# A decoder layer in fp32 on one core: the second weight unit in halves, later returns of turned rows, and a last norm whose shift rows come from TensorE

## The chip, the cores and the metric

The kernel runs on one core of a Trainium2 chip. The metric is the device time of one execution in microseconds (us). A core has a matmul engine (TensorE, PE in the profile; PEld is its weight load), three engines for elementwise work (VectorE or DVE, ScalarE or ACT, GpSimd or POOL) and a queue engine (SyncE, SP) that mostly issues DMA transfers. Each engine runs its own list of instructions in order and waits on semaphores that other engines or transfers raise.

## The reference

One layer, batch 1, 256 tokens, model width 2048, all in float32. Cut to what the change touches:

```python
h = layer_norm(ALPHA*h + 0.5*swiglu(h, ffn1...), ln1_g, ln1_b)
mix = mixer(h, ...)      # w_in, latent attention (MLA) and differential attention, gates, w_out
h = layer_norm(ALPHA*h + mix, ln2_g, ln2_b)
h = layer_norm(ALPHA*h + 0.5*swiglu(h, ffn2...), ln3_g, ln3_b)

def swiglu(x, w_gate, w_up, w_down): return (silu(x @ w_gate) * (x @ w_up)) @ w_down
def layer_norm(x, g, b):
    mu = mean(x); var = mean((x - mu)**2)
    return (x - mu) * rsqrt(var + 1e-5) * g + b
# inside the mixer
c_q, c_kv, k_r, dq, dk, dv, gate_mla, gate_diff = split(h @ w_in)
q = (rms_norm(c_q) @ w_uq) ...; k_nope = rms_norm(c_kv) @ w_uk; v = rms_norm(c_kv) @ w_uv
```

## The kernel before, in words

The 256 tokens are two blocks `b` of 128. A product of two fp32 matrices is done as three fp32r matmuls of 128x128 by 128x512 (`triple`, L208 to L210): high part times high part, high times low of the weight, low of the activation times high. High and low parts are made on the way: a weight comes by DMA on the SP queue into a `raw` tile (four buffers) or an `sraw` tile, ACT casts it (the high part, L154), DVE subtracts the cast from the raw values (the low part, L155), and the two land in a pair of tiles of a ring named `wring`. Activations pass through the same `split`, as `x`, `xs`, `cn`, `y`, `h`. PE's first use of a weight unit, L208, waits for the cast; the second, L209, for the subtraction. A unit is 128x1024, two k tiles.

The products of the FFNs and the mixer are mostly taken by `Hybrid`, with seven block products in the place of eight. In these DVE also forms sums of weight blocks (L428) and of products, and ACT copies PSUM banks into `snap` tiles (L385, L386), from which DVE later takes differences (L1194, with dk's rows as `dkTr`).

Work beside the matmuls is put into a list by `later(n, fn)`: it is emitted when n more units have been emitted (`tick`). After that a scheduler orders the instructions of each engine; `tc.issue_after(i)` holds what it wraps behind instruction i. The order on each engine is therefore fixed when the program is built.

A transposition of 128x512 rows goes by DVE (`blocks`, L715), four POOL-issued writes to DRAM (`turn`, L717), and one POOL-issued read (`turned`, L729, 256 KB), after which ACT copies or casts it. In the mixer the rows of the two latents wait in DRAM from an early stage on; `c_back` (L1227) reads them back as four `turned` tiles, and `cn.put` splits them (`cn`). `turned`, `blocks`, `gp` and the rows of `dkT` share one pool of six temporary tiles, so that each transfer into one waits until a former user is done.

The first projection (gate and up of FFN1) loads x transposed between its weight units: `load_x` (L1401) brings one quad of k tiles and one token block, 256 KB. Its first unit is loaded and split in two halves (`parts`).

The norms are a class. `evac` adds a bank to `z`, `bn_stats` and `bn_aggr` give mean and variance (`mv`), and `rstd` makes 1/sqrt in six small steps (`ve`, `sd` on ACT, `w`, `y`, `t`, `f`). In the last norm (no `cols`), `center(c)` does (z - mean) * g on a chunk of 512 columns (L833), a second pass does z * f + bias (L839), and each chunk is stored by SP at once (L1433). Chunks of z live in `z`, gains and biases in `gb`. LN2, whose `gained` brings ln1's gain and bias rows (`gp`) and applies them to the residual, runs beside w_out.

Of the kernel before, what the change touches and what calls it, by code (L numbers as in the profile page):

```python
# [18 lines left out]
P = 128  # L19
# [11 lines left out]
G = 2  # L31
# [28 lines left out]
def layer_kernel(ctx: ExitStack, tc: tile.TileContext, a: dict, out: bass.AP):  # L60
# [89 lines left out]

    cast, lows, fetched = [None], [None], [None]

# [59 lines left out]
    def project(w, x, k_tiles, width, done, k0=0, hook=None, between=None, norm=None, free=(3, 7)):  # L212
# [526 lines left out]
    class LayerNorm:  # L739
        def __init__(self, scale, residual, g, bt, each, x=None, cols=None, at=((0, 2, 4, 6), (8, 11, 14, 17)), ahead=None, pending=None, due=(), past=None):  # L740
# [45 lines left out]
            for n in range(4):  # L786
                later(at[0][n], lambda n=n: rows(n // 2, n % 2))
                if cols is None:
                    later(at[1][n], lambda n=n: vector(n // 2, n % 2))
            self.stats = [small.tile([P, 4, 6], F32, tag="bn", name=nm("bn"), bufs=4) for _ in range(2)]  # L790

# [32 lines left out]
        def apply(self, b):  # L824
# [3 lines left out]
            if self.cols is None:  # L828
# [3 lines left out]
                def center(c):  # L832
                    V.scalar_tensor_tensor(out=zs[c], in0=zs[c], scalar=mv[:, 0:1], in1=gs[c],  # L833
                                           op0=ALU.subtract, op1=ALU.mult)
                r = rstd(mv[:, 1:2], LN_EPS, 1, lambda: center(0))
                for c in range(4):
# [294 lines left out]
    def mixer(x):  # L1131
# [92 lines left out]
        def c_back():  # L1224
            for key, src in turns.items():
                back[key] = tmp_tile([P, 512], "turned")
                nc.gpsimd.dma_start(back[key], src)  # L1227
# [186 lines left out]
    def keep(i):  # L1414
        def each(b, c, z):
# [16 lines left out]
    ffn(2, h2, a["gu2"], a["dn2"], res[1], a["ln3_g"], a["ln3_b"],  # L1432
        lambda b, c, z: nc.sync.dma_start(out[b * P:(b + 1) * P, c * 512:(c + 1) * 512], z), norm=ln,  # L1433
        pending=(a["ln2_g"], a["ln2_b"]))
# [85 lines left out]
```

## Time and profile before

| | |
|---|---|
| median of 3 runs | 1966.95 us (1966.76 to 1967.80) |
| profiled execution | 1969.03 us |
| its span | 1967.3 us, so 1.7 us lie outside it |
| PE busy | 1951.7 us, 99% of the span, 8760 matmuls |
| DVE, ACT, POOL busy | 1777.8, 1249.7, 309.3 us |
| DMA | 488.83 MB, 248 GB/s over the span |
| mean granted clock of TensorE | 0.998 |

A row of a timeline reads: start in us from the span's start, duration, engine, source line, operation, output<-inputs, how many in a row, and in brackets the idle time of that engine just before and what ended it. Rows of the list of waits name who waited, for whom, the total in us, how many times, and the longest.

### The profile page before, as it was taken

The page shows a single profiled execution, that of the slowest core. Times are in us where ns is not written, and L with a number is a line of the kernel's source. Part 1 is how long each engine was busy: PE and PEld are TensorE (multiplying, and loading weights), DVE is VectorE, ACT ScalarE, POOL GpSimd, SP SyncE. Part 2 cuts the span into 40 slices and gives each one's busy share as a digit, 9 for nine tenths or more (in the row PEclk, how much of TensorE's full clock was granted, in tenths as well). Part 3 has the DMA queues.
Part 4 walks back from the last instruction along what each step waited for, and adds up shares of the span by engine and source line. Part 5 has one row for each costly group of instructions (what it writes and reads, how often), then busy time and mean ns, then how long its engine had stood idle before and what let it go on. Part 6 is the DMA issues. An engine that isn't in the chain of part 4 may idle for free.

```text
span 1967.3 us, 25772 instructions
## 1 busy us (share of the span) xinstructions
PE 1951.7 (99%) x8760; PEld 1618.2 (82%) x8760; DVE 1777.8 (90%) x2183; ACT 1249.7 (64%) x1634; POOL 309.3 (16%) x531
## 2 busy tenths in 40 slices
PE   9999999999999999999999999999999999999997
PEld 8888888888888898888888887888888888888886
DVE  7999999998998879988987676789999999999986
ACT  6666766676655666666667654556676666765661
POOL 0112111122100010102241530001211112210000
PEclk9999999999999999999999999999999999999999
DMA  8978888878776666767685788678888878787773
GB/s 315 285 227 262 268 261 247 259 234 306 271 238 214 208 223 248 246 223 262 203 248 196 236 295 274 198 261 255 255 267 264 250 238 271 251 314 236 277 233 121
DMA packets 149779, 488.83 MB, mean 248 GB/s; under 512 B 21600, under 2 KB 21648, under 8 KB 149648
## 3 DMA queue, kind: packets, MB, share of 16 engines
q1 hardware_dynamic: 119088, 401.13, 59.5%
q0 software_dynamic: 30560, 86.07, 16.8%
q8 instruction: 68, 1.11, 0.2%
q14 instruction: 63, 0.52, 0.1%
HBM read 456.71 MB, written 30.41 MB: 248 GB/s over the span
## 4 chain that ended last, share of the span: by engine, by line
PE 92%; DMA 3%; DVE 1%; issue 1%; ACT 1%; POOL 1%; SPq 0%; DVEq 0%; POOLq 0%; ACTq 0%
PE mm L209 29%; PE mm L208 29%; PE mm L210 29%; DMA turned<-turn 1%; DMA gate<-gates 1%; PE tr L210 1%; PE tr L209 1%; PE tr L208 1%; DMA turn<-blocks 0%; POOL turn L717 0%; PE tr L671 0%; ACT wring L154 0%; DMA raw<-in_wgd_dram 0%; DMA raw<-in_gu_dram 0%; PE tr L1322 0%
## 5 line engine op out<-in xcount | busy, mean ns | idle before, releaser
L154 ACT CAST wring<-raw 128x1024 fp32r<-128x1024 f32 (+2 forms) x467 | 481.9, 1037 | 322.3 <-PE mm L210 236.7
L155 DVE TENSOR_TENSOR wring<-raw,wring 128x1024 fp32r<-128x1024 f32 (+2 forms) x467 | 557.4, 1201 | 91.7 <-ACT wring L154 89.4
L154 ACT CAST wring<-sraw 128x1024 fp32r<-128x1024 f32 x436 | 453.0, 1052 | 201.9 <-DVE sraw L428 85.7
L155 DVE TENSOR_TENSOR wring<-sraw,wring 128x1024 fp32r<-128x1024 f32 x436 | 520.7, 1219 | 23.6 <-ACT wring L154 20.7
L208 PE MATMUL mm<-wring,h 128*128 128x512 f32 (+2 forms) x1248 | 480.9, 385 | 0.0
L210 PE MATMUL mm<-wring,h 128*128 128x512 f32 (+2 forms) x1248 | 480.3, 385 | 0.0
L209 PE MATMUL mm<-wring,h 128*128 128x512 f32 (+2 forms) x1248 | 480.0, 385 | 0.0
L208 PE MATMUL mm<-wring,xs 128*128 128x512 f32 x776 | 302.2, 389 | 0.6 <-ACT snap L385 0.6
L209 PE MATMUL mm<-wring,xs 128*128 128x512 f32 x776 | 301.9, 389 | 0.0
L210 PE MATMUL mm<-wring,xs 128*128 128x512 f32 x776 | 301.9, 389 | 0.0
L208 PEld LDWEIGHTS mm<-wring,h 128*128 128x128 f32 x1248 | 234.5, 188 | 46.9 <-ACT h L154 0.6
L209 PEld LDWEIGHTS mm<-wring,h 128*128 128x128 f32 x1248 | 234.5, 188 | 46.5 <-DVE wring L155 0.4
L210 PEld LDWEIGHTS mm<-wring,h 128*128 128x128 f32 x1248 | 234.4, 188 | 46.5 <-DVE h L155 0.7
L428 DVE TENSOR_TENSOR sraw<-sraw,sraw 128x1024 f32<-128x1024 f32 x168 | 199.2, 1219 | 2.0 <-DMA sraw<-in_wgm_dram 1.2
L208 PEld LDWEIGHTS mm<-wring,xs 128*128 128x128 f32 x776 | 145.7, 188 | 31.2 <-ACT snap L385 1.0
L210 PEld LDWEIGHTS mm<-wring,xs 128*128 128x128 f32 x776 | 145.7, 188 | 30.2
L209 PEld LDWEIGHTS mm<-wring,xs 128*128 128x128 f32 x776 | 145.7, 188 | 30.1
L717 POOL DMA_DIRECT2D hT<-blocks x176 | 96.8, 562 | 367.0 <-DVE blocks L715 366.0
L209 PE MATMUL mm<-wring,x 128*128 128x512 f32 x336 | 130.8, 389 | 0.5 <-DVE wring L155 0.5
L208 PE MATMUL mm<-wring,x 128*128 128x512 f32 x336 | 130.8, 390 | 0.0
L210 PE MATMUL mm<-wring,x 128*128 128x512 f32 x336 | 130.6, 389 | 0.0
L430 POOL DMA_DIRECT2D sraw<-in_gu_dram x40 | 35.5, 889 | 371.3 <-DVE sraw L428 288.3
(310 smaller groups left out, 2286.7 us busy)
## 6 DMA issues: line engine op xcount, KB each, us to landing
sraw<-in_gu_dram SPq DMA_DIRECT2D x160, 512.0 KB, 5.2
raw<-in_gu_dram SPq DMA_DIRECT2D x159, 512.0 KB, 4.9
raw<-in_dn_dram SPq DMA_DIRECT2D x140, 512.0 KB, 4.7
sraw<-in_gu_dram POOLq DMA_DIRECT2D x40, 512.0 KB, 7.1
sraw<-in_dn_dram SPq DMA_DIRECT2D x36, 512.0 KB, 5.2
eraw<-in_gu_dram SPq DMA_DIRECT2D x64, 256.0 KB, 5.8
raw<-in_w_out_dram SPq DMA_DIRECT2D x32, 512.0 KB, 4.3
hraw<-hT POOLq DMA_DIRECT2D x56, 256.0 KB, 5.8
```

The source lines that it names most:

```text
L154: cast[0] = S.copy(hi, src)
L155: lows[0] = V.tensor_tensor(out=lo, in0=src, in1=hi.bitcast(F32), op=ALU.subtract)
L208: PE.matmul(o, xh, wh, start=first, stop=False, skip_group_check=again)
L209: PE.matmul(o, xh, wl, start=False, stop=False, skip_group_check=again)
L210: PE.matmul(o, xl, wh, start=False, stop=last, skip_group_check=again)
L428: last = V.tensor_tensor(out=R[src][i], in0=R[src][i], in1=R[add[1]][i], op=ALU.add)
L430: nc.gpsimd.dma_start(R["12"][s], source("22", s), accum_op=ALU.add)
L717: nc.gpsimd.dma_start(to.rearrange("(g r) (i f) -> i r g f", g=4, i=4)[i], t[32 * i:32 * (i + 1), :].rearrange("r (g f) -> r g f", g=4))
```

## The change

It has four parts.

1. **Head.** The second weight unit of the first projection (j = 1) is loaded and split in halves too. The load of unit 3 is held behind the x load that was emitted last (`placed`).
2. **Mixer.** The read-back of the latents (`c_back`) moves from 6 to 12 units ahead, and the four splits into `cn` from 12 to 18 units (plus 4 and 2 per tile, as before).
3. **LN2.** The residual rows and the first two `gained` chunks come one unit later; the use of the first chunk's rows is due after 3 and 5 units, not 4 and 6.
4. **Tail.** For token block 1 of the last norm, chunks 0 and 1 of z are multiplied by the gain during FFN2 (`gained_ahead`). The last norm then needs, for these chunks, z*g * r minus a row (mean * r * g - bias). That row comes from TensorE: `ends` puts ln3's gain and bias, high and low parts, into rows of a 64-row tile (`gb_rows`); ACT builds a column pair (mean * r, and -1), PE transposes it, ACT copies it (`lhs`), and one matmul per chunk makes the shift in a PSUM bank. DVE then does one pass per chunk, from PSUM. Chunks go in the order 3, 2, 0, 1; chunk 1 in two halves, and the last half's store is issued from ACT's queue.

```diff
-            parts = [slice(i * width, (i + 1) * width) for i in range(G)] if between is not None and j == 0 else [slice(0, G * width)]
+            parts = [slice(i * width, (i + 1) * width) for i in range(G)] if between is not None and j < 2 else [slice(0, G * width)]
...
-                for c in parts:
-                    fetched[0] = nc.sync.dma_start(st["raw"][:, c], w[j][:, c])
+                with tc.issue_after(placed[0].ins) if between is not None and j == 3 else nullcontext():
+                    for c in parts:
+                        fetched[0] = nc.sync.dma_start(st["raw"][:, c], w[j][:, c])
...
-        nc.sync.dma_start(raw, a["xT"][q, b])
+        placed[0] = nc.sync.dma_start(raw, a["xT"][q, b])
...
-                later(4, lambda: use(0))
-                later(6, lambda: use(1))
+                wait = 3 if past is not None and c == 0 else 4
+                later(wait, lambda: use(0))
+                later(wait + 2, lambda: use(1))
...
+                def ends():
+                    raw = act_tile([P, 1024], F32, "gbraw")
+                    self.gb_rows = act_tile([P, 1024], F32R, "gbr")
+                    self.pair = tmp_tile([P, 64], "pair", F32R)
+                    V.memset(raw[0:64, :], 0.0)
...
+                    for i, v in ((0, g), (1, g), (2, bt), (32, g), (33, bt)):
+                        nc.gpsimd.dma_start(raw[i:i + 1, :], v[0:1, 0:1024])
+                    def parted():
+                        S.copy(self.gb_rows[0:64, :], raw[0:64, :])
+                        V.tensor_tensor(out=self.gb_rows[32:64, :], in0=raw[32:64, :],
+                                        in1=self.gb_rows[32:64, :].bitcast(F32), op=ALU.subtract)
+                    later(5, parted)
+                def gained_ahead(c):
+                    z = self.z[1][0][:, c * 512:(c + 1) * 512]
+                    with tc.issue_after(lows[0].ins):
+                        V.tensor_tensor(out=z, in0=z, in1=self.gb[0][0][:, c * 512:(c + 1) * 512], op=ALU.mult)
+                later(at[1][1] + 1, ends)
+                for c in range(2):
+                    later(at[1][0] + 5 + c, lambda c=c: gained_ahead(c))
...
+                if b == 1:
+                    r = rstd(mv[:, 1:2], LN_EPS, 1, lambda: center(3))
+                    s = sm(1, "s")
+                    S.activation(s, mv[:, 0:1], AF.Identity, scale=r)
+                    S.copy(self.pair[:, 0:33:32], s.to_broadcast([P, 2]))
+                    S.activation(self.pair[:, 1:2], self.pair[:, 0:1].bitcast(F32), AF.Identity, scale=-1.0, bias=s)
+                    t = tr_bank()
+                    PE.transpose(t[0:64, 0:P], self.pair.bitcast(F32), ident)
+                    lhs = tmp_tile([P, P], "lhs", F32R)
+                    S.copy(lhs[0:64, :], t[0:64, 0:P])
+                    shifts = [mm_bank() for _ in range(2)]
+                    for c in range(2):
+                        PE.matmul(shifts[c], lhs[0:64, :], self.gb_rows[0:64, c * 512:(c + 1) * 512], start=True, stop=True)
+                    for c in (3, 2, 0, 1):
...
-        later(6, c_back)
+        later(12, c_back)
...
-                later(12 + 4 * i + 2 * b, lambda i=i, b=b: cn.put(i, b, turned(back[i, b])))
+                later(18 + 4 * i + 2 * b, lambda i=i, b=b: cn.put(i, b, turned(back[i, b])))
...
-    ln = LayerNorm(1.0, res[0], a["ln2_g"], a["ln2_b"], keep(1), h2, a["ln2_cols"], ((1, 3, 11, 13), ()), 1,
-                   (a["ln1_g"], a["ln1_b"]), (2, 7, 14, 21), lambda: yq.made[3, 1])
+    ln = LayerNorm(1.0, res[0], a["ln2_g"], a["ln2_b"], keep(1), h2, a["ln2_cols"], ((2, 4, 11, 13), ()), 1,
+                   (a["ln1_g"], a["ln1_b"]), (3, 8, 14, 21), lambda: yq.made[3, 1])
```

Where instructions stand now, at three places.

The first is DVE in the head, around weight units 9 (`wring_103`, low part), 10 (`wring_121`) and 11 (`wring_119`); `sg` and `hb` are the gate's evacuation of the first projection, `xs` the activations' block sums. DVE before the change:

```order
L155 TENSOR_TENSOR wring_105<-raw_318,wring_104 128x1024
L155 TENSOR_TENSOR xs_337<-fa_288,xs_336 128x1024
L155 TENSOR_TENSOR wring_121<-raw_356,wring_120 128x1024
L870 TENSOR_TENSOR hb_306<-mm_136,sg_304 128x256
L155 TENSOR_TENSOR wring_103<-raw_340,wring_102 128x1024
L870 TENSOR_TENSOR hb_316<-mm_148,sg_314 128x256
L155 TENSOR_TENSOR wring_119<-raw_376,wring_118 128x1024
L155 TENSOR_TENSOR xs_373<-fb_289,xs_372 128x1024
L155 TENSOR_TENSOR wring_117<-raw_392,wring_116 128x1024
```

DVE at the same place after the change:

```order
L155 TENSOR_TENSOR wring_105<-raw_321,wring_104 128x1024
L155 TENSOR_TENSOR wring_121<-raw_359,wring_120 128x1024
L919 TENSOR_TENSOR hb_309<-mm_136,sg_307 128x256
L919 TENSOR_TENSOR hb_319<-mm_148,sg_317 128x256
L155 TENSOR_TENSOR xs_340<-fa_291,xs_339 128x1024
L155 TENSOR_TENSOR wring_119<-raw_379,wring_118 128x1024
L155 TENSOR_TENSOR wring_103<-raw_343,wring_102 128x1024
L155 TENSOR_TENSOR wring_117<-raw_395,wring_116 128x1024
L155 TENSOR_TENSOR xs_376<-fb_292,xs_375 128x1024
```

Unit 9's low part stood ahead of the second `hb`, of unit 11 and right behind the first `hb`; now the second `hb`, `xs_340` and unit 11 stand ahead of it.

The second is POOL's queue in the mixer, at the products of dv; `turn_7366`, `7409`, `7463`, `7470` (before) and `turn_7369`, `7412`, `7458`, `7465` (after) are dk's four row tiles on their way to `dkT`. POOL before the change:

```order
L717 DMA turn_7366<-blocks_7367 32x4x128 x4
L1227 DMA turned_7433<-turn_5559 128x512
L717 DMA turn_7409<-blocks_7410 32x4x128 x4
L1227 DMA turned_7435<-turn_5626 128x512
L1227 DMA turned_7437<-turn_6324 128x512
L1227 DMA turned_7439<-turn_6443 128x512
L729 DMA turned_7441<-turn_7366 128x512
L717 DMA turn_7463<-blocks_7464 32x4x128 x4
L717 DMA turn_7470<-blocks_7471 32x4x128 x4
L729 DMA turned_7499<-turn_7409 128x512
L729 DMA turned_7521<-turn_7463 128x512
L729 DMA turned_7523<-turn_7470 128x512
```

POOL at the same place after the change:

```order
L718 DMA turn_7369<-blocks_7370 32x4x128 x4
L730 DMA turned_7436<-turn_7369 128x512
L718 DMA turn_7412<-blocks_7413 32x4x128 x4
L730 DMA turned_7494<-turn_7412 128x512
L718 DMA turn_7458<-blocks_7459 32x4x128 x4
L718 DMA turn_7465<-blocks_7466 32x4x128 x4
L730 DMA turned_7516<-turn_7458 128x512
L730 DMA turned_7518<-turn_7465 128x512
L1276 DMA turned_7537<-turn_5562 128x512
L1276 DMA turned_7539<-turn_5629 128x512
L1276 DMA turned_7541<-turn_6327 128x512
L1276 DMA turned_7543<-turn_6446 128x512
```

The four reads of the latents (L1227, now L1276) stood among the writes of dk's rows and now stand behind all of them and their reads. With `dkT` made earlier, the scheduler also moved one matmul of the attention scores (L1299, `tr_7782`) forward on PE, from a later stage to between two of dv's products:

```order
L209 MATMUL mm_7475<-wring_119,xs_5877 128x512
L210 MATMUL mm_7475<-wring_118,xs_5877 128x512
L1299 MATMUL tr_7782<-dkT_7032,dqT_6758 128x128
L208 MATMUL mm_7499<-wring_116,xs_5766 128x512
L209 MATMUL mm_7499<-wring_117,xs_5766 128x512
L210 MATMUL mm_7499<-wring_116,xs_5767 128x512
L208 MATMUL mm_7499<-wring_116,xs_5766 128x512
L209 MATMUL mm_7499<-wring_117,xs_5766 128x512
```

Before, this piece of PE's list held the same products without the L1299 row, which then stood some 180 rows later.

The third is DVE at the end, for token block 1 of the last norm (`mm_15605` and `mm_15606` are the shift banks). DVE before the change:

```order
L826 BN_AGGR mv_15564<-bn_13735 128x2
L690 TENSOR_SCALAR ve_15566<-mv_15564 128x1
L833 SCALAR_TENSOR_TENSOR z_13981<-z_13981,mv_15564,gb_15261 128x512
L696 TENSOR_SCALAR w_15570<-mv_15564 128x1
L700 RECIPROCAL y_15573<-sd_15568 128x1
L833 SCALAR_TENSOR_TENSOR z_13981<-z_13981,mv_15564,gb_15261 128x512
L703 SCALAR_TENSOR_TENSOR t_15575<-y_15573,w_15570 128x1
L833 SCALAR_TENSOR_TENSOR z_14759<-z_14759,mv_15564,gb_15308 128x512
L709 SCALAR_TENSOR_TENSOR f_15577<-t_15575,y_15573 128x1
L833 SCALAR_TENSOR_TENSOR z_14759<-z_14759,mv_15564,gb_15308 128x512
L839 SCALAR_TENSOR_TENSOR z_13981<-z_13981,f_15577,gb_15358 128x512 x2
L839 SCALAR_TENSOR_TENSOR z_14759<-z_14759,f_15577,gb_15403 128x512 x2
```

DVE at the same place after the change:

```order
L852 BN_AGGR mv_15582<-bn_13738 128x2
L691 TENSOR_SCALAR ve_15584<-mv_15582 128x1
L859 SCALAR_TENSOR_TENSOR z_14762<-z_14762,mv_15582,gb_15311 128x512
L697 TENSOR_SCALAR w_15588<-mv_15582 128x1
L701 RECIPROCAL y_15591<-sd_15586 128x1
L704 SCALAR_TENSOR_TENSOR t_15593<-y_15591,w_15588 128x1
L710 SCALAR_TENSOR_TENSOR f_15595<-t_15593,y_15591 128x1
L879 SCALAR_TENSOR_TENSOR z_14762<-z_14762,f_15595,gb_15419 128x512
L859 SCALAR_TENSOR_TENSOR z_14762<-z_14762,mv_15582,gb_15311 128x512
L879 SCALAR_TENSOR_TENSOR z_14762<-z_14762,f_15595,gb_15419 128x512
L879 SCALAR_TENSOR_TENSOR z_13984<-z_13984,f_15595,mm_15605 128x512
L879 SCALAR_TENSOR_TENSOR z_13984<-z_13984,f_15595,mm_15606 128x256 x2
```

Two of four centering passes are gone, none stands between `y` and `f` any more, and the chunks 3 and 2 come first.

More of the change, by code (lines that the diff above doesn't have):

```diff
@@ L149, in at @@
             return self.tiles[k // 8, b][which][:, k % 8, :]
-    cast, lows, fetched = [None], [None], [None]
+    cast, lows, fetched, placed = [None], [None], [None], [None]
     def split(hi, lo, src):
@@ L789, in __init__ @@
                     later(at[1][n], lambda n=n: vector(n // 2, n % 2))
+            if cols is None:
+                def ends():
[3 more added lines that the diff above has]
+                    V.memset(raw[0:64, :], 0.0)
+                    V.memset(self.pair.bitcast(F32), 0.0)
+                    V.memset(self.pair[:, 2:34:31].bitcast(F32), -1.0)
+                    for i, v in ((0, g), (1, g), (2, bt), (32, g), (33, bt)):
[12 more added lines that the diff above has]
+                    later(at[1][0] + 5 + c, lambda c=c: gained_ahead(c))
             self.stats = [small.tile([P, 4, 6], F32, tag="bn", name=nm("bn"), bufs=4) for _ in range(2)]
@@ L834, in center @@
                                            op0=ALU.subtract, op1=ALU.mult)
+                if b == 1:
[12 more added lines that the diff above has]
+                    for c in (3, 2, 0, 1):
+                        if c == 2:
+                            with tc.issue_after(last.ins):
+                                center(2)
+                        for o in (slice(0, 512),) if c != 1 else (slice(0, 256), slice(256, 512)):
+                            last = V.scalar_tensor_tensor(out=zs[c][:, o], in0=zs[c][:, o], scalar=r,
+                                                          in1=(bs[c] if c > 1 else shifts[c])[:, o], op0=ALU.mult,
+                                                          op1=ALU.add if c > 1 else ALU.subtract)
+                            self.each(b, c, zs[c][:, o], o)
+                    return
                 r = rstd(mv[:, 1:2], LN_EPS, 1, lambda: center(0))
@@ L1432, in layer_kernel @@
     ffn(2, h2, a["gu2"], a["dn2"], res[1], a["ln3_g"], a["ln3_b"],
-        lambda b, c, z: nc.sync.dma_start(out[b * P:(b + 1) * P, c * 512:(c + 1) * 512], z), norm=ln,
+        lambda b, c, z, o=slice(0, 512): (nc.scalar if o.start else nc.sync).dma_start(
+            out[b * P:(b + 1) * P, c * 512 + o.start:c * 512 + o.stop], z), norm=ln,
         pending=(a["ln2_g"], a["ln2_b"]))
```

## The prediction

> **What bounds the kernel now.** I read the page first, then the list of PE's waits, then the windows of the stages that the change touches, and then their timelines.
>
> ```profile
> span 1967.3 us, 25772 instructions
> PE 1951.7 (99%) x8760; PEld 1618.2 (82%) x8760; DVE 1777.8 (90%) x2183; ACT 1249.7 (64%) x1634; POOL 309.3 (16%) x531
> ```
>
> PE is busy 99% of the span. No part of the change takes a matmul away (it adds three small ones at the end), so only the 15.6 us in which PE does not work can be won. The list of PE's waits names the longest of them inside the kernel; two windows, late in FFN2 and in the tail, follow:
>
> ```profile
> PE tr L671 <- DVE diff L1376: 1.8, 1, 1.8
> ...
> PE mm L208 <- ACT snap L385: 0.6, 1, 0.6
> PE mm L209 <- DVE wring L155: 0.5, 1, 0.5
> ...
> 1870.00:1952.00 82.00, 82.00 (x363) 67.89 (x362) 65.29 (x73) 39.21 (x42) 2.12 (x4) 1.00 0.55 182
> ...
> 1960.00:1964.00 4.00, 0.00 (x0) 0.00 (x0) 3.88 (x7) 0.00 (x0) 0.00 (x0) 0.50 0.32 118
> ```
>
> The four parts aim at the wait on `wring` (head), on `snap` (mixer), on `diff` (LN2) and the tail after PE's last matmul. In the windows the numbers after the length are the busy times of PE, PEld, DVE, ACT and POOL; the 1.00 or 0.50 near the end is TensorE's granted clock. The sum below is made against the profiled execution, 1969.03 us (span 1967.3 and 1.7 outside it); the median is 1966.95, 2.1 less, and I apply the differences to the median.
>
> **Head.** What the halves are to cure:
>
> ```profile
> 7.99 1.05 ACT L154 CAST wring<-raw 128x1024 fp32r<-128x1024 f32 x1 [0.84 <-DMA raw<-in_gu_dram]
> 9.07 2.49 DVE L155 TENSOR_TENSOR wring<-raw,wring 128x1024 fp32r<-128x1024 f32 x2 [1.20 <-ACT wring L154]
> 9.20 0.63 PE L208 MATMUL mm<-wring,x 128*128 128x512 f32 x2
> 9.26 1.05 ACT L154 CAST wring<-raw 128x1024 fp32r<-128x1024 f32 x1 [0.22 <-DMA raw<-in_gu_dram]
> 10.36 0.50 PE L209 MATMUL mm<-wring,x 128*128 128x512 f32 x1 [0.53 <-DVE wring L155]
> ```
>
> Unit 1 arrives at 7.99; its cast takes 1.05 and the subtraction some 1.24 more (2.49 for two), so PE's L209 starts at 10.36. The second L208 began at 9.43 (two in 0.63 us, a start every 0.23), and L209 would have been due at 9.66: 0.70 is lost, and 0.1 more in a slow restart. With halves, the low part of the first half follows its own arrival after about half of both durations, before PE is due. This wait goes: −0.8.
>
> Two things turn up instead. First, the x loads. The new SP order puts units 3, 4 and 5 ahead of x quad 2, where before only units up to 4 were ahead of it.
>
> ```profile
> 13.88 0.62 ACT L154 CAST x<-xraw 128x512 fp32r<-128x512 f32 x1 [1.21 <-DMA xraw<-in_xT_dram]
> 15.74 1.22 DVE L155 TENSOR_TENSOR wring<-raw,wring 128x1024 fp32r<-128x1024 f32 x1
> ```
>
> Unit loads arrive 1.27 us apart (7.99 and 9.26 above), so quad 2 comes at about 15.15, not 13.88. ACT waits there, unit 4's cast is behind it on ACT, and unit 4's low part, made 15.74 to 16.96 before, ends at about 18.23. PE used it at 18.45; with 0.8 less lost ahead of it, and one L208 more hoisted in front, it is due at 17.7 to 17.8. That is a wait of about 0.5 (0 if the transfers catch up, 0.8 if the last x half is late too).
>
> Second, unit 9. Its low part now stands on DVE behind the second `hb`, `xs_340` and unit 11, and that `hb` waits for an ACT `sg` that waits for the last matmul of the first gate bank:
>
> ```profile
> 27.95 0.38 ACT L863 ACTIVATE sg<-mm 128x256 f32<-128x256 f32 x1 [0.16 <-PE mm L210]
> 28.91 0.42 DVE L870 TENSOR_TENSOR hb<-mm,sg 128x256 f32<-128x256 f32 x1
> 29.31 1.22 DVE L155 TENSOR_TENSOR wring<-raw,wring 128x1024 fp32r<-128x1024 f32 x1
> ...
> 32.05 0.39 PE L209 MATMUL mm<-wring,x 128*128 128x512 f32 x1
> ```
>
> Before, unit 9 was made 29.31 to 30.53 and first used at 32.05: a slack of 1.5. After: let that last matmul start at t. `sg` runs t+0.43 to t+0.81 (0.43 is a matmul's 0.39 and a step), `hb` takes 0.40 to the next start (28.91 to 29.31), then two passes of 128x1024 at 1.13 from start to start, and unit 9's own 1.22: ready at t+4.7. PE has 14 matmuls from t to unit 9's L209, 14 times 0.2265 = 3.2. So PE waits about 1.5, and since `sg` is tied to PE itself, earlier delays do not give slack back. Bounds: 0 (DVE reaches the rows sooner than I chain them) to 2.0. I take 1.5, since every link has a row.
>
> Head: −0.8 + 0.5 + 1.5 + 0.1 for the restarts = **+1.3** (−0.8 to +2.2).
>
> **Mixer.** Here a read of turned rows holds ACT, and everything behind it:
>
> ```profile
> 932.99 1.64 POOL L717 DMA_DIRECT2D turn<-blocks  x3
> ...
> 944.22 1.63 POOL L1227 DMA_DIRECT2D turned<-turn  x3
> ...
> turned<-turn POOLq DMA_DIRECT2D x5, 256.0 KB, 4.7
> turn<-blocks POOLq DMA_DIRECT2D x8, 64.0 KB, 3.4
> ...
> 949.45 0.62 ACT L154 CAST cn<-turned 128x512 fp32r<-128x512 f32 x1 [2.60 <-DMA turned<-turn]
> ...
> 953.14 0.69 DVE L1194 TENSOR_TENSOR dkTr<-mm,snap 128x512 f32<-128x512 f32 x1
> ...
> 953.86 0.59 ACT L386 COPY snap<-mm 128x512 f32<-128x512 f32 x1 [0.85 <-DVE dkTr L1194]
> ...
> 958.03 0.58 ACT L385 COPY snap<-mm 128x512 f32<-128x512 f32 x1
> ...
> 947.81 0.39 PE L210 MATMUL mm<-wring,h 128*128 128x512 f32 x1
> 948.22 0.50 PE L208 MATMUL mm<-wring,h 128*128 128x512 f32 x1
> ...
> 957.67 0.39 PE L210 MATMUL mm<-wring,h 128*128 128x512 f32 x1
> 958.66 0.50 PE L208 MATMUL mm<-wring,xs 128*128 128x512 f32 x1 [0.61 <-ACT snap L385]
> ```
>
> The two rows that end in 4.7 and 3.4 give the median time from issue to landing in 930 to 952. `cn` waits 2.60 for a read issued after 944.22; the casts behind it are late, DVE's `dkTr` with them, then the two snaps, and PE's start at 958.66 comes 0.99 after the one before instead of 0.23: 0.76 lost, and 0.1 at the restart. The same between 947.81 and 948.22: 0.2 and 0.1, where a PSUM bank waits for the `dkTr` before. Moving the reads out of this chain lets `dkTr` run as soon as PE has the products, so the snaps fall before PE asks. That is 1.0 to 1.2 to be had. What is late next: `cn` itself, which POOL now issues behind eight `turn` writes at 0.55 each and their landing. I get 956 for the issue and, with the 4.7 us that such a read took here, 961 for the first cast; PE wants the casts queued behind it only at about 967. DVE is nearly full from 938 to 960, and I allow 0.2 for a low part that comes late. I take **−0.9** (−1.2 to +0.5).
>
> **LN2.** The stall is the longest, but the change does not touch what ends it:
>
> ```profile
> 1176.64 6.99 DMA turned<-turn
> ...
> 1186.65 0.69 DVE L1376 TENSOR_TENSOR diff<-diff,gate 128x512 f32<-128x512 f32 x1
> ...
> 1187.49 0.63 PE L671 MATMUL tr<-ident,diff 128*128 128x128 f32 x4 [1.84 <-DVE diff L1376]
> ```
>
> A read that took 6.99 us frees ACT and then DVE from 1183.63 on, DVE reaches the difference at 1186.65, and PE its first transpose of it at 1187.49. On SP one pair of `gp` loads moves behind a weight load, on DVE and ACT one multiplication moves past a weight split. The read was issued at 1176.64, and what stands ahead of it in the transfers is the same. **0** (−0.5 if less traffic shortens the read, +0.5 if a weight split is delayed).
>
> **Tail.**
>
> ```profile
> 1958.19 0.74 DVE L833 SCALAR_TENSOR_TENSOR z<-z,mv,gb 128x512 f32<-128x512 f32 x1
> 1958.30 0.20 ACT L692 ACTIVATE sd<-ve 128x1 f32<-128x1 f32 x1 [7.95 <-DVE ve L690]
> ...
> 1960.42 0.15 DVE L709 SCALAR_TENSOR_TENSOR f<-t,y 128x1 f32<-128x1 f32 x1
> 1960.49 0.74 DVE L833 SCALAR_TENSOR_TENSOR z<-z,mv,gb 128x512 f32<-128x512 f32 x1
> 1961.15 2.73 DVE L839 SCALAR_TENSOR_TENSOR z<-z,f,gb 128x512 f32<-128x512 f32 x4
> ...
> out_dram<-z SPq DMA_DIRECT2D x8, 256.0 KB, 2.1
> ```
>
> Before: four centering passes, the small steps between them, and four second passes, about 0.66 from start to start, end at 1963.88. After: one centering pass from 1958.19, then `w`, `y`, `t`, `f` in a row, `f` ready at about 1959.45; then second pass of chunk 3, centering and second pass of chunk 2, chunk 0, and chunk 1 in two halves of about 0.4. On DVE alone this ends at 1959.5 + 4 × 0.66 + 0.8 = 1962.9. But chunk 0 needs its shift: from `f`, three small ACT steps at 0.2 (the `sd` row), a transpose (at most 0.63, the row at 1187.49 holds four), an ACT copy of at most 0.4 and a matmul. With the clock at 0.50, as the window 1960 to 1964 has it, that matmul costs what one of 0.62 us in the head costs:
>
> ```profile
> 6.20 0.62 PE L208 MATMUL mm<-wring,x 128*128 128x512 f32 x1
> ```
>
> That makes 1959.45 + 0.6 + 0.5 + 0.3 + 0.6 and some 0.3 in steps = 1961.75, while DVE is free for chunk 0 at 1961.5. So DVE ends at about 1963.15, 0.7 sooner. The last store is half as large; its 2.1 us shrink by some 0.2. Tail: **−0.9** (−1.3 to −0.2; the worse end if ACT's first store or the small ops take 0.2 longer each).
>
> The Trainium skill (TensorE: Matmul & The Clock Gate, section "Part 1: The HAM clock gate") says that TensorE falls to half of its clock once it has been idle for one activity window of about 3.4 us; it speaks against putting matmuls here. The trace agrees: PE's last matmul ends at 1956.3, and the 1960 to 1964 window shows 0.50. An estimate by its latencies is 0.61 us cold and 0.38 warm for a 512-column matmul; with the clock still full the tail would come out at about −1.1 and the sum at −0.7.
>
> The work that `ends` and `gained_ahead` put into FFN2 (two multiplications of 0.7, a memset, a cast and a half subtraction, none over 1.22) I cost at nothing: in 1870 to 1952 above DVE has 16.7 us idle and PE none. Without that cover PE would lose up to 4 us.
>
> **Sum.** +1.3 − 0.9 + 0 − 0.9 = −0.5 on 1969.03 makes 1968.5; on the median, 1966.4.
>
> **Rivals.**
> (a) *The head does not pay.* If DVE reaches unit 9 in time and quad 2 catches up, the head is −0.8, and with mixer and tail at −1.0 and −0.9 the time is 1964.3. For it: each head wait is a sum of single steps against about 1.5 and 0.7 of slack. Against it: the `sg` link is tied to PE.
> (b) *Slower.* PE now does one score matmul (L1299) between dv's products, due at about 943.9, and in order. It needs `dkT`'s first tile: its read is issued when the `turn` writes, the last of them given out at about 934.1, have landed 3.4 later, about 937.5; at 4.7 us it is in at 942.2, and after a copy of 0.6 PE is served by 943.5. At the 6.99 us of the row above it would be 945.1: PE waits 1.2, and later reads are as slow, so that ACT stalls on the second tile and the mixer's gain goes. From a latency of about 5.2 us on it decides. Head +1.3, mixer +1.2, tail −0.7: 1968.8.
> (c) *The clock rule weighs more.* The three PE operations and their hops take so long that chunk 0 waits 0.6 more, and the tail gives −0.3: 1967.0.
> (d) *A part does not do what it says.* The mixer's snap is late for another reason (DVE is nearly full there), its gain is 0.1: 1967.2.
>
> **Chances.** Forecast 0.5; (a) 0.2; (b) 0.14; (c) 0.08; (d) 0.08. None of these alone passes 0.2% (3.9 us, about what a measurement of this kernel can tell from no change). To be faster by more, (a) and a shorter LN2 stall must meet: 0.03. Slower by more needs (b) with a head at its upper end, or FFN2 without its cover: 0.06. The range reaches from (a) to (b): 1964.3 to 1968.8.
>
> **What would show it.** Head right: no wait at L209 at 10.36, ACT idle before x quad 2 near 15.1, a PE wait of some 0.5 near 18 and one of some 1.5 near 31, both named DVE `wring`. Mixer right: no PE wait on `snap`, ACT idle of under 1 us before `cn`. LN2 right: the L671 wait still 1.5 to 2.2. Tail right: `f` near 3.1 us after the last matmul, last DVE pass 6.8 after it, granted clock 0.50 on three PE operations. Wrong: a total below 1964 or above 1969, a wait on L1299, or waits in FFN2.

## The result

Over 22 runs each the changed kernel took a median of 1971.24 us (1969.41 to 1973.07), the kernel before 1967.74 (1966.39 to 1969.16). The ratio is 1.0018, with a 95% interval of 1.0012 to 1.0024: slower by 3.5 us (2.4 to 4.7). The forecast was 0.5 us faster, with a range up to 1968.8. The profiled execution of the changed kernel took 1971.83 us, its span is 1970.0.

PE's list of waits after the change, columns as before:

```profile
span 1970.0 us, 25797 instructions
...
PE tr L868 <- ACT pair L866: 4.1, 1, 4.1
PE mm L209 <- DVE wring L155: 2.1, 4, 1.3
PE tr L1160 <- DVE p L1308: 1.7, 2, 1.0
PE tr L98 <- DVE zero L96: 1.1, 1, 1.1
PE mm L208 <- ACT wring L154: 0.8, 1, 0.8
PE mm L873 <- ACT lhs L870: 0.3, 1, 0.3
```

The waits on `diff` and on `snap` are gone. In their place stand waits on weight parts (`wring`) and on softmax rows (`p`, transposed at L1160 in the attention). What makes the 1.7 us on `p` was not taken apart; with the mixer part alone a wait of 0.4 stands there. The 4.1 us at L868 lie behind the last product, where PE has nothing else to do. Next, the windows of the head and of the mixer of the changed kernel, of the head of the kernel before, and of LN2's stage of both (the number behind the length is PE's busy time):

```profile
0.00:50.00 50.00, 46.29 (x199) 37.74 (x200) 38.08 (x48) 31.74 (x40) 1.54 (x9) 1.00 0.83 299
945.00:1000.00 55.00, 54.59 (x239) 43.69 (x238) 46.98 (x55) 36.30 (x48) 12.14 (x23) 1.00 0.64 213
1160.00:1200.00 40.00, 40.00 (x186) 33.14 (x185) 33.91 (x42) 19.41 (x24) 10.20 (x19) 1.00 0.91 296
```
```profile
0.00:50.00 50.00, 48.41 (x213) 40.48 (x214) 39.79 (x48) 32.70 (x41) 3.05 (x11) 1.00 0.88 317
...
1160.00:1200.00 40.00, 38.16 (x176) 31.35 (x176) 31.47 (x39) 19.25 (x24) 6.99 (x13) 1.00 0.85 291
```

PE works 2.1 us less in the head, and 1.8 more beside LN2. First three rows of the head before the change (SP from 20 us on, then ACT), then the head after it, by the timelines of SP, ACT, DVE and PE:

```profile
20.87 8.48 SPq L235 DMA_DIRECT2D raw<-in_gu_dram  x4
...
25.43 1.06 ACT L154 CAST wring<-raw 128x1024 fp32r<-128x1024 f32 x1 [0.49 <-DMA raw<-in_gu_dram]
26.51 1.28 ACT L863 ACT_TABLE_LOAD   x1
```
```profile
22.88 4.47 SPq L236 DMA_DIRECT2D raw<-in_gu_dram  x2
...
15.88 0.62 ACT L154 CAST x<-xraw 128x512 fp32r<-128x512 f32 x1 [2.19 <-DMA xraw<-in_xT_dram]
...
27.38 1.05 ACT L154 CAST wring<-raw 128x1024 fp32r<-128x1024 f32 x1 [2.86 <-DMA raw<-in_gu_dram]
28.34 1.05 ACT L154 CAST xs<-fa 128x1024 fp32r<-128x1024 f32 x1
29.41 1.28 ACT L912 ACT_TABLE_LOAD   x1
30.70 0.66 ACT L912 ACTIVATE sg<-mm 128x256 f32<-128x256 f32 x2
...
31.11 0.76 DVE L919 TENSOR_TENSOR hb<-mm,sg 128x256 f32<-128x256 f32 x2 [1.24 <-ACT sg L912]
31.79 1.22 DVE L155 TENSOR_TENSOR xs<-fa,xs 128x1024 fp32r<-128x1024 f32 x1
32.92 3.49 DVE L155 TENSOR_TENSOR wring<-raw,wring 128x1024 fp32r<-128x1024 f32 x3
...
19.03 0.50 PE L209 MATMUL mm<-wring,x 128*128 128x512 f32 x1 [0.30 <-DVE wring L155]
...
32.08 0.39 PE L210 MATMUL mm<-wring,x 128*128 128x512 f32 x1
33.29 0.73 PE L208 MATMUL mm<-wring,x 128*128 128x512 f32 x2 [0.82 <-ACT wring L154]
35.33 0.50 PE L209 MATMUL mm<-wring,x 128*128 128x512 f32 x1 [1.31 <-DVE wring L155]
```

x quad 2 is cast at 15.88, where before it was 13.88. With it DVE finishes the low parts of units 4 to 6 about 2 us later, and their raw buffers come free that much later: unit 10's load is issued at 22.88, before at 20.87. Its weights come only at 27.38, before at 25.43, and ACT, which has that cast in front, waits 2.86 for them. Behind it stand `xs`, the table load (which ACT does ahead of its first `sg`) and both `sg`. DVE starts the two `hb` at 31.11, and unit 9's cast and low part come after all of these, and behind those of unit 11. PE starts unit 9 at 33.29 and its L209 at 35.33, where they were due at 32.3 and, two matmuls on, at 32.8.

### The profile page after: what moved, and what is told of

Same layout as the page of the kernel before. It is cut to its first block, busy times and chain, and to the rows that moved or that the text cites. A ratio compares the mean times of both kernels' runs of the same rounds, so it can differ in the third digit from the quotient of the medians.

```text
span 1970.0 us, 25797 instructions
## 1 busy us (share of the span) xinstructions
PE 1955.0 (99%) x8763; PEld 1618.5 (82%) x8763; DVE 1779.8 (90%) x2189; ACT 1252.5 (64%) x1640; POOL 311.9 (16%) x536
## 4 chain that ended last, share of the span: by engine, by line
PE 95%; DMA 2%; DVE 1%; ACT 1%; issue 1%; POOL 0%; SPq 0%; DVEq 0%; ACTq 0%; POOLq 0%
PE mm L210 30%; PE mm L209 30%; PE mm L208 30%; PE tr L209 1%; PE tr L208 1%; PE tr L210 1%; DMA turned<-turn 1%; DVE wring L155 1%; DMA raw<-in_gu_dram 1%; PE tr L672 0%; ACT wring L154 0%; PE tr L1299 0%; DMA xraw<-in_xT_dram 0%; POOL turn L718 0%; PE tr L1371 0%
## 5 line engine op out<-in xcount | busy, mean ns | idle before, releaser
L209 PE MATMUL mm<-wring,h 128*128 128x512 f32 (+2 forms) x1248 | 480.4, 385 | 0.4 <-DVE wring L155 0.3
L209 PE MATMUL mm<-wring,xs 128*128 128x512 f32 x776 | 302.1, 389 | 0.0
L209 PEld LDWEIGHTS mm<-wring,h 128*128 128x128 f32 x1248 | 234.5, 188 | 47.9 <-DVE wring L155 2.0
L209 PEld LDWEIGHTS mm<-wring,xs 128*128 128x128 f32 x776 | 145.7, 188 | 30.4 <-DVE wring L155 0.2
L209 PE MATMUL mm<-wring,x 128*128 128x512 f32 x336 | 131.1, 390 | 1.8 <-DVE wring L155 1.8
```

What stands on the lines that cost most here:

```text
L209: PE.matmul(o, xh, wl, start=False, stop=False, skip_group_check=again)
```

## The experiments

The four parts touch different stretches of the instruction lists, and alone each makes the same change there as together. So they could be run one by one.

**Each part alone.** Edits: the kernel before with part 1, 2, 3 or 4 of the change, as in the diff above.

> The kernel before with the head part alone (second unit in halves, unit 3's load behind the x load). Theory from the changed kernel's trace (its idle time before PE's matmuls in the first 50 us is 4.2 us against 1.0): all of that is this part's own doing, so the time goes up by about 3.2 us, PE waits at unit 4 (about 0.5) and at unit 9 (about 2.5 in two pieces). The prediction as put down: up by 1.3. Rival: the order of the head comes from the other parts too, and alone the wait at the second unit goes and nothing takes its place: down by 0.8.

> The mixer part alone (read-back of the latents 12 units ahead, splits 18). Theory from the changed kernel's trace (950 to 1050 us: 5.0 us of idle time against 3.25): the two waits on a PSUM bank and on a snap go, but ACT's later casts are late, PE waits at three low or high parts of dv's and later products (about 1.1 together) and more at two transposes of softmax rows (about 1.5): time up by 1.4 us. The prediction as put down: down by 0.9. Rival: the extra waits come from the 4 us by which the head delays PE there; alone the part gives -0.9 or so.

> The LN2 part alone (residual rows and first gain rows one unit later). Theory A: the part itself takes the 1.85 us wait of PE on the difference away, since fewer transfers run beside the read of turned rows that ends late: down by about 2.0 us. Theory B (as predicted, 0): the read's chain is earlier than everything the part moves, and it was the later arrival of PE, or chance in the transfers, that removed the wait in the changed kernel: the wait stays at 1.5 to 2.2 us, time within 0.5 us.

> The tail part alone (gain ahead for two chunks, shift rows by PE). Theory from the changed kernel's trace (from the start of the last FFN matmul to the end of the span 10.9 us against 11.3): down by 0.4 us, with no new wait in FFN2. The prediction as put down: down by 0.9. Rival: the work put into FFN2 costs PE something there, and the time goes up.

| part alone | median, us (11 runs) | ratio to before (1967.63) | interval |
|---|---|---|---|
| head | 1971.77 | 1.0022 | 1.0013 to 1.0030 |
| mixer | 1968.00 | 1.0001 | 0.9992 to 1.0010 |
| LN2 | 1967.67 | 1.0002 | 0.9993 to 1.0011 |
| tail | 1967.45 | 0.9998 | 0.9989 to 1.0007 |

The head part alone makes the loss: 4.1 us by the medians, 2.6 to 5.9 by the interval. For the other three the intervals reach about 2 us to either side, so their times alone decide between none of the expectations; the four differences add to 4.3, the whole change gave 3.5. Of LN2's two expectations B has the time right, but not the wait: B let it stay, and with LN2's part alone it is gone (PE is busy for all of 1160 to 1200). Nor is its absence LN2's doing, as A has it: the 1.8 us wait on `diff` is absent with the head, mixer or tail part alone too, none of which touches LN2. Of sixteen profiles a wait on `diff` stands in two, the kernel before (1.8) and `best3` below (1.0), and `best3` has LN2's part. These are LN2's stage with the head part alone and in `best3`:

```profile
1160.00:1200.00 40.00, 40.00 (x186) 33.13 (x185) 34.68 (x42) 19.43 (x24) 10.40 (x20) 1.00 0.93 306
```
```profile
1160.00:1200.00 40.00, 38.99 (x181) 32.03 (x180) 31.63 (x39) 19.11 (x24) 6.54 (x12) 1.00 0.88 298
```

**The head taken apart.** `h_halves` is j < 2 alone, `h_pin` the pin on unit 3 alone. `h_pin35` is the head part with unit 5 pinned too; `h_unit9` is the head part with the casts of units 10 and 11 held behind that of unit 9 (`all_casts` collects the casts of `split` in order: number 22 is unit 9's, 23 and 25 are those of units 10 and 11).

```diff
h_pin35:
-                with tc.issue_after(placed[0].ins) if between is not None and j == 3 else nullcontext():
+                with tc.issue_after(placed[0].ins) if between is not None and j in (3, 5) else nullcontext():
h_unit9:
-        cast[0] = S.copy(hi, src)
+        with tc.issue_after(all_casts[21].ins) if len(all_casts) in (22, 24) else nullcontext():
+            cast[0] = S.copy(hi, src)
...
+        all_casts.append(cast[0])
```

> The kernel before with the second unit in halves and nothing else; in the lists of the engines one load, one cast and one subtraction become two, all else stands as before. Theory: the head's loss is the pin's (unit 3's load behind the x load), not the halves'; alone the halves take away the wait at the second unit (0.7 to 0.8 us) and the time goes down by about 0.8 us or stays, with unit 9 in time. Rival: the smaller transfers themselves cost, and the time goes up by a part of the 4 us that the head part showed.

> Unit 3's load behind the x load, without the halves. Theory: this moves x quad 2 behind unit 5's load on SP, so x comes about 1.3 us late, the raw buffers come free about 2 us late, unit 10 arrives 2 us late, and ACT's first sg, which now stands behind unit 10's cast, holds DVE and so unit 9: a PE wait of about 2.6 us in two pieces near 32 and one of 0.4 near 18. Time up by 3.3 to 4.3 us. Rival: only both together do it; the pin alone costs under 1 us.

> The head part (halves and the pin on unit 3's load) with unit 5's load held behind the x loads as well. On SP x quad 2 then stands ahead of unit 5's load, as it did before the change, and unit 9's low part stands right behind the first hb again. Theory (x quad 2 behind unit 5's load is what starts the chain over the raw buffers to unit 10 and the first sg): nearly all of the head's 4 us go, the time is within 1 us of the kernel before, no PE wait near 18 and none over 0.3 near 32. Rival (the pin on unit 3 alone, or any change of order in the head, costs): 2 us or more stay.

> The head part as in the change (halves, unit 3 pinned, x quad 2 behind unit 5's load), with the casts of units 10 and 11 held behind unit 9's cast on ACT, so that unit 9's cast and low part stand ahead of units 10 and 11 and of the second sg and hb again. Theory (the place in the lists is what costs at unit 9; the late x quad costs only unit 4): PE's wait of 2.6 to 2.8 us near 32 goes, the one of 0.4 to 0.5 near 18 stays; the time is 0 to 1 us over the kernel before, not 4. Rival (the late raw buffers decide: unit 10 or a later unit simply waits in unit 9's place): a wait of over 1.5 us stays near 32 to 38, the time is 2 us or more over.

| head variant | median, us | before beside it | ratio | interval |
|---|---|---|---|---|
| halves alone | 1967.40 | 1967.71 | 1.0001 | 0.9992 to 1.0010 |
| pin alone | 1972.45 | 1967.71 | 1.0024 | 1.0014 to 1.0033 |
| halves, units 3 and 5 pinned | 1967.09 | 1968.03 | 0.9994 | 0.9985 to 1.0002 |
| head part, unit 9 ahead of 10 and 11 | 1967.84 | 1967.83 | 1.0001 | 0.9992 to 1.0009 |

The pin costs it all (4.7 us alone); the halves neither cost nor bring anything that can be told apart. With unit 5's load held behind x quad 2 as well, the loss is gone. `h_unit9` separates the two things that this moves together: x quad 2 stays late, only the lists at unit 9 are put back, and again the loss is gone. The head windows of `h_pin`, `h_pin35` and `h_unit9`, and for `h_unit9` the late quad, the first `sg`, which waits for PE again, and the wait at unit 4 that is kept:

```profile
0.00:50.00 50.00, 45.66 (x189) 36.53 (x190) 35.87 (x45) 31.09 (x38) 1.55 (x9) 0.97 0.84 292
```
```profile
0.00:50.00 50.00, 48.94 (x217) 41.30 (x218) 40.75 (x51) 33.70 (x42) 3.42 (x11) 1.00 0.86 315
```
```profile
0.00:50.00 50.00, 48.39 (x212) 40.12 (x213) 39.95 (x49) 32.83 (x42) 2.94 (x11) 1.00 0.85 305
...
15.48 0.62 ACT L156 CAST x<-xraw 128x512 fp32r<-128x512 f32 x1 [2.47 <-DMA xraw<-in_xT_dram]
...
28.47 0.38 ACT L867 ACTIVATE sg<-mm 128x256 f32<-128x256 f32 x1 [0.62 <-PE mm L213]
...
18.62 0.50 PE L212 MATMUL mm<-wring,x 128*128 128x512 f32 x1 [0.50 <-DVE wring L157]
```

So the late x quad alone costs about 0.7 at unit 4 (18.62 against 17.9), and the order of the lists at unit 9 the rest. `h_unit9` changes two things in that order: unit 10's cast goes behind `sg`, and unit 9 goes ahead of the second `sg` and `hb` and of unit 11. Which of the two would do alone was not run.

**The mixer.** Edit on top of the mixer part:

```diff
-                later(18 + 4 * i + 2 * b, lambda i=i, b=b: cn.put(i, b, turned(back[i, b])))
+                later(26 + 4 * i + 2 * b, lambda i=i, b=b: cn.put(i, b, turned(back[i, b])))
```

> The mixer part with the splits into cn another 8 units later (26 in the place of 18), so that ACT meets them after their reads have landed. Theory (ACT's wait of 6 us for the first read, with weight casts behind it, ate the gain): no PE wait on a snap near 958, none of the three on a low part near 966 to 978, idle time from 950 to 1050 us down by about 2 us against the part alone, time about 1 us under the kernel before. Rival: DVE is full there in any order and other low parts come late: idle time about as with the part alone, time as before.

Measured: 1966.15 us against 1968.03, ratio 0.9990 (0.9982 to 0.9999): faster by 1.9 (0.2 to 3.5). The waits that the mixer part alone had are in POOL's, ACT's and PE's timelines of `p_mixer`; behind them the time from issue to landing of the five reads of 955 to 975, and the window; then `m_put`, with its first `cn` and its window:

```profile
948.59 0.56 POOL L729 DMA_DIRECT2D turned<-turn  x1 [3.66 <-ACT snap L386]
949.14 4.36 POOL L717 DMA_DIRECT2D turn<-blocks  x8
...
957.56 0.56 POOL L729 DMA_DIRECT2D turned<-turn  x1 [3.14 <-DMA turn<-blocks]
958.11 2.12 POOL L1227 DMA_DIRECT2D turned<-turn  x4
...
964.87 0.62 ACT L154 CAST cn<-turned 128x512 fp32r<-128x512 f32 x1 [6.03 <-DMA turned<-turn]
...
967.76 0.50 PE L209 MATMUL mm<-wring,h 128*128 128x512 f32 x1 [0.74 <-DVE wring L155]
...
turned<-turn POOLq DMA_DIRECT2D x5, 256.0 KB, 7.2
...
945.00:1000.00 55.00, 53.67 (x235) 43.06 (x234) 46.84 (x59) 37.03 (x52) 13.14 (x25) 1.00 0.68 217
```
```profile
974.16 0.62 ACT L154 CAST cn<-turned 128x512 fp32r<-128x512 f32 x1
...
945.00:1000.00 55.00, 55.00 (x247) 45.34 (x247) 49.62 (x63) 38.44 (x54) 16.54 (x31) 1.00 0.72 232
```

With the splits at 18 units ACT stands 6.03 us before a read, with weight casts behind it; at 26 it meets them with no wait (it still stands 4.19 before a read of dk's rows, until 964.05). From 950 to 1050 us PE's idle time goes from 1.8 us with the mixer part to 0.3; about 2 less was expected. One such window would not show a gain over the kernel before: in eleven profiles with the mixer as before, PE's idle time from 945 to 1000 runs from 0 (in `best`) to 1.5 us. It is 0 in all three profiles with the splits at 26 (`m_put` and, below, `best3` and `best4`). The size of the gain rests on the medians.

**The tail.** On top of the tail part, `t_warm` puts 15 matmuls on the zero tile ahead of the transposition of the shift; `t_sp` issues all stores from SP. Each of the two was executed once, so that only their profiles can be read and not their times.

```diff
t_warm:
+                    idle = tr_bank()
+                    for _ in range(15):
+                        PE.matmul(idle[:, 0:P], zero, zero, start=True, stop=True)
                     t = tr_bank()
t_sp:
-        lambda b, c, z, o=slice(0, 512): (nc.scalar if o.start else nc.sync).dma_start(
+        lambda b, c, z, o=slice(0, 512): nc.sync.dma_start(
```

> The tail part alone with 15 matmuls of 128 columns on the zero tile between the last FFN2 matmul and the transpose of the shift, so that TensorE is not idle there; they write a bank that nobody reads. Theory (half clock): with the clock at full speed the two 512-column matmuls take about 0.4 us and start 0.23 apart, not 0.6 and 0.6; the shift of chunk 0 is ready about 0.2 to 0.3 us sooner, DVE starts chunk 0 at 5.7 us after the start of the last FFN matmul, not at 6.0, and the end comes 0.2 to 0.3 sooner. Rival: the chain of small ACT steps sets it, or the clock falls anyway: the end moves by less than 0.1.

> The tail part alone with all stores on SP's queue. Theory (the queue does not matter, a store of 128 KB takes as long as one of 256): issue of the last store to its landing 2.1 to 2.2 us, as from ACT's queue, and the end within 0.1 of the tail part alone. Rival: ACT's first store is the slow one, and SP gives 0.2 back.

The tail's end in the changed kernel (PE's transposition and shift matmuls, the window of the shift, the last two stores), in the tail part alone, and in `t_warm` (PE's shift matmuls, then DVE's last three passes):

```profile
1963.59 0.42 PE L868 MATMUL tr<-ident,pair 128*64 128x128 f32 x1 [4.12 <-ACT pair L866]
1964.36 1.22 PE L873 MATMUL mm<-gbr,lhs 64*128 64x512 f32 x2 [0.35 <-ACT lhs L870]
...
1963.00:1966.00 3.00, 1.64 (x3) 0.63 (x3) 2.67 (x5) 0.75 (x3) 0.00 (x0) 0.50 0.31 117
...
out_dram<-z SPq DMA_DIRECT2D x1, 128.0 KB, 2.2
out_dram<-z ACTq DMA_DIRECT2D x1, 128.0 KB, 2.2
```
```profile
1960.36 1.22 PE L871 MATMUL mm<-gbr,lhs 64*128 64x512 f32 x2 [0.35 <-ACT lhs L868]
1961.19 1.53 DVE L877 SCALAR_TENSOR_TENSOR z<-z,f,mm 128x512 f32<-128x512 f32 x3 [0.18 <-PE mm L871]
```
```profile
1959.22 0.73 PE L874 MATMUL mm<-gbr,lhs 64*128 64x512 f32 x2 [0.35 <-ACT lhs L871]
1959.79 1.53 DVE L880 SCALAR_TENSOR_TENSOR z<-z,f,mm 128x512 f32<-128x512 f32 x3
```

With PE kept at work the two shift matmuls take 0.73 together, not 1.22, and DVE no longer waits for them. From the start of the last FFN2 matmul to the end of the span it is 11.4 us before, 10.9 with the tail part (alone and in the change), 10.7 with `t_warm`, 11.0 with `t_sp`. Two more profiles with the matmuls on the zero tile (`best3` and `best4`, below) have 10.6, and one more without them (`best`) 11.0, with ACT's queue. So the issuing queue makes no difference that can be seen, and a store of 128 KB takes 2.2 us from either, as long as one of 256 (2.1).

**Put together.** `best` is the halves, LN2's and the tail's part; `best3` the halves, the mixer with splits at 26, LN2's part and the tail with `t_warm`; `best4` is `best3` with units 3 and 5 pinned.

> The halves without the pin, LN2's part and the tail's part, the mixer as before. Theory (the parts add): -0.8 for the halves, 0 for LN2, -0.4 for the tail: about 1.2 us under the kernel before. Rival: the halves gain nothing, since the arrival of the first loads differs by more than a microsecond from one execution to the next: about -0.4.

> The halves without the pin, the mixer part with splits 26 units ahead, LN2's part, and the tail's part with 15 matmuls on the zero tile in the idle time. If the parts add: 0 to -0.8 for the halves, -1.0 for the mixer, -0.65 for the tail: 1.6 to 2.4 us under the kernel before. Rival: the mixer's gain is not there: 0.6 to 1.0 under.

> Halves with units 3 and 5 pinned, the mixer part with splits 26 units ahead, LN2's part, and the tail's part with matmuls in the idle time. If the parts add (from their medians: -0.9, -1.9, 0, -0.2 to -0.65): 3.0 to 3.5 us under the kernel before. Rival: the parts do not add, about as best3, 2.6 under.

| | median, us | before beside it | ratio | interval |
|---|---|---|---|---|
| best | 1967.55 | 1967.71 | 0.9997 | 0.9989 to 1.0006 |
| best3 | 1965.38 | 1968.03 | 0.9989 | 0.9980 to 0.9998 |
| best4 | 1965.69 | 1967.83 | 0.9987 | 0.9978 to 0.9996 |

`best` is not told apart from the kernel before. `best3` and `best4` are faster than the kernel before, by 2.7 and 2.1 us in the medians (intervals 0.4 to 3.9 and 0.8 to 4.3), and not told apart from each other. Their medians are 5.6 to 5.9 under that of the changed kernel, which did not run beside them. The 3.0 to 3.5 expected of `best4` is not reached by the median, though its interval still holds it.

## Why the prediction was wrong

**Head: the term that decided.** Forecast +1.3, measured +4.1. The two new waits stood where the prediction had them. Unit 9's was mis-sized: 1.0 at the first use, 1.5 at the second and two restarts make 2.7, forecast 1.5. The step that failed is "since `sg` is tied to PE itself": it was tied to ACT. ACT's list has unit 10's cast and the table load ahead of `sg`. Before the change that cast came early enough for the first `sg` to wait only for PE; now unit 10's load left late (22.88), because the late x quad held unit 4 and with it the raw buffers. The prediction priced the late quad at unit 4 and did not follow it through the buffers to unit 10.

The size fits. Counted back by the forecast's 14 matmuls from unit 9's L209, the last matmul of that bank started at 29.6, and the second `sg` was due 0.43 later, at 30.0. It ran at about 31.0. From its end (31.4) to the end of unit 9's low part (35.3, the second of the three from 32.92) it took 3.9 us, as forecast. So 1.5 of the wait is the order on DVE, which the prediction had right, and 1.0 is ACT's late `sg`, which it had not. `h_unit9` shows that the late quad reaches unit 9 only through the order of the lists there: the quad is about as late, and 0.7 at unit 4 is all it costs.

Unit 4's wait had the forecast size (0.46 and a restart of 0.1, forecast 0.5) by luck. Quad 2 was cast at 15.88, not at 15.15, and PE was due for unit 4's low part at 18.6, not at 17.7 to 17.8: both came 0.7 to 0.8 later than forecast, and the difference stayed.

The credit of −0.8 for the halves failed too. They do take away the wait at the second unit, but the arrival of the first loads already differs much from one execution to the next: in the profiles with unchanged head order PE's busy time in the first 50 us runs from 46.74 (LN2's part alone) to 48.48, and with the halves alone the median moved by no more than 0.3. The sum was made against one execution whose head was among the good ones and whose LN2 was the worst seen. The two waits make 3.3 us; that lies inside the interval of the head part alone, and what makes the rest of its 4.1 is not known, though a fall of the clock in some executions (last section) may be a part of it.

**Mixer.** The waits removed were named rightly, and so was what comes late next, `cn`. The step that failed is its time: the first cast was put at 961, with PE wanting the casts behind it at 967. With the mixer part alone it came at 964.87, and PE waited 0.74 at 967.76 for a low part whose cast stood behind it. Two terms were too small. The reads were issued from 958.11 on, not at 956: POOL came to its eight writes only at 949.14, after a wait of 3.66 us (the profile names an ACT `snap`, but the four writes given out from 941.77 to 944.9 may have been landing still, and which of the two ended it is open), and then waited for their landing until 957.56. And the first read took 6.8 us from its issue to the cast, not 4.7; the median of the five issued there was 7.2. In time the forecast is not refuted: −0.9, measured +0.4 with an interval of −1.6 to +2.0. It is −1.9 once the splits stand later, which supports the reading that the late `cn` ate a gain that was there. The rival with the score matmul did not decide: no wait on L1299 is in the list.

**LN2.** Forecast 0, measured 0.0 with an interval of −1.4 to +2.2. The reason given, that the change does not touch what ends the wait, is not contradicted; its sign, a wait still of 1.5 to 2.2, did not come. The wait itself was a sample: it stands in two of sixteen profiles, so that it is missing from the changed kernel's profile is not the change's doing.

**Tail.** Forecast −0.9, measured −0.4 to −0.5 in the profiles; the medians (−0.2) cannot tell. `f` is ready as forecast, 3.6 us after the last matmul's start. The terms that were off are the last store, for which the forecast took off 0.2 with no row that shows it (from the end of DVE's last pass to the end of the span it is 3.3 us now and 3.4 before), and the passes from `f` to the end, 0.4 longer: chunk 0 began 6.1 us after the last matmul's start and not 5.8, and DVE's last pass ended at 7.6 and not at 7.2. The rule of the half clock (the Trainium skill, TensorE: Matmul & The Clock Gate, "Part 1: The HAM clock gate") held here: after 4.1 us of idle PE was granted 0.50 in the window of the shift. The tail is about 0.3 shorter where PE does not idle.

The work put into FFN2 was indeed covered: no PE wait in FFN2 appears in the list. The outcome, slower, is that of rival (b), but not by its mechanism: the head made the loss.

## What to carry to other kernels

When a change moves one transfer, follow it through every buffer that waits for its consumers, and then ask which short instruction stands behind the last of them in the list of an engine. Here that was `sg`, and holding two casts back gave the 4 us back. A wait seen in one profile is a sample: before a term is built on it, compare with other executions, since here three of the four targets (head, mixer, LN2) differed by 1.5 to 1.8 us from one profile to another of kernels with that stage unchanged. To move a wait on a transfer, move the consumer as well as the read.

## What the runs showed of the hardware

The pin alone showed the clock fall in the middle of the kernel. After the waits at unit 9, eight matmuls of `h_pin` start 0.43 us apart, at a granted clock of 0.53 over that stretch, though PE had only stood idle for 0.56 and 1.31 us, far less than the 4.1 us ahead of the tail's half clock:

```profile
33.79 0.73 PE L208 MATMUL mm<-wring,x 128*128 128x512 f32 x2 [0.56 <-ACT wring L154]
...
36.26 0.63 PE L210 MATMUL mm<-wring,x 128*128 128x512 f32 x1
36.69 0.63 PE L208 MATMUL mm<-wring,x 128*128 128x512 f32 x1
...
32.00:35.80 3.80, 1.96 (x8) 0.98 (x6) 3.80 (x6) 3.47 (x4) 0.00 (x0) 1.00 0.62 207
35.80:39.30 3.50, 3.47 (x9) 2.70 (x10) 3.50 (x4) 3.50 (x5) 0.00 (x0) 0.53 0.91 248
```

At 0.2265 per matmul those eight starts would take 1.6 us less, beside the 2.3 us that the two waits cost. The length of the waits does not decide it: the changed kernel stood idle longer at the same place (0.82 and 1.31), and its clock stayed at 1.00. What does decide it is not shown.

It is not a single case. The mean granted clock of a run, given to three places, reads 0.997 in 5 of the 11 runs of `h_pin`, in 3 of the 11 of the head part alone and in 2 of the 22 of the changed kernel, the three kernels that wait at unit 9, and in no run of another kernel whose clock is on record; a fall to 0.53 for 3.5 us of some 1970 lowers the mean by 0.0008. In `h_pin` these five runs take 1973.5 us in the mean, the other six 1971.5.
